# One 128x128 inverse for both heads of a pair: four separate tile chains become one, and the products walk the four 32x32 corners in turn

## Chip, cores and metric

The kernel runs on one core of a Trainium2 chip. The metric is the device time of one execution in microseconds (us); lower is better. TensorE multiplies, VectorE (DVE) and ScalarE (ACT) move and combine tiles, GpSimd (POOL) does small elementwise work, SyncE (SP) issues the DMA transfers. The profile also gives TensorE's granted clock as a share of its upper level: 1.0 is 2.4 GHz and 0.5 is 1.2 GHz.

## The reference, cut to what matters

Two decoder layers on 256 tokens of width 1024. The first one has a Gated DeltaNet mixer with 8 heads, cut into chunks of C tokens (64 in the reference; the kernel takes 128, so a head has two chunks). In every chunk of every head a unit lower triangular matrix is inverted:

```
L = jnp.where(strict, jnp.einsum('bhnid,bhnjd->bhnij', kb, k) * decay, 0.0)
eye = jnp.eye(C, dtype=f32)
T = lax.linalg.triangular_solve(eye + L, jnp.broadcast_to(eye, L.shape),
                                left_side=True, lower=True, unit_diagonal=True)
u = jnp.einsum('bhnij,bhnjd->bhnid', T, v * beta[..., None])
w = jnp.einsum('bhnij,bhnjd->bhnid', T, kb * jnp.exp(gc)[..., None])
```

The rest (causal convolutions, the state that runs from chunk to chunk, memory attention, the ConvGLU, the sparse attention of the second layer) is not touched. All of it is in float32; the large products split each operand into a rounded high part and a low part.

## The kernel before

**How the program comes to its order.** The Python code only records operations; every recorded call has line 389, so the profile is read by tile names and not by lines. The class `Sched` then sets the order on each engine: a list scheduler with a cost for each operation (`_cost`), a priority by place in the code, and a limited number of buffers of each kind. A `with PE.group():` block is one operation to it and stays together. Each engine runs its own list strictly in order; when the count or cost of an operation changes, the lists of all engines may change far around it.

**The work around the inverse.** `gdn_pair(p)` handles two heads (`e` is 0 or 1) with two chunks each (`t` is 0 or 1), for four pairs. Each pair goes through three stages that the list `"dd0dddddd01021321323"` interleaves with those of other pairs: projections, convolution and the matrix `LL` (128x128 for each chunk); the inverse; and the walk over the chunks. `pj` and `pf` are the accumulators of ordinary projections (128x256 products in high and low parts), which the scheduler sets between the dependent steps of a pair. The weights of `pf` (memory keys and values) arrive as `mr`, ScalarE rounds them to `mh`, VectorE makes the rest `ml`.

**The inverse of a 128x128 chunk.** The 16x16 diagonal blocks are inverted row by row on VectorE and GpSimd (`DD`, `tm`), sent through DRAM and come back as `cd`. From there the inverse is built up in three steps, each of two products with a copy between them:

1. 32x32: `D32` holds the inverses of the four 32x32 diagonal blocks, first without their inner corner; two products and one VectorE operation on the result complete them (first product `mx<-D,LL`, `X` is made on VectorE, second product `mx<-D,X` and `mx<-X,D`, the second of these for the transposed copy).
2. 64x64: six ScalarE copies put `D` into the tile `full`; product `mx<-D,LL` (off-diagonal 32x32 blocks), two copies to `X`, product `mx<-X,D` and `mx<-D,X`, three scaled copies into `full`.
3. 128x128: product `mx<-full,LL` (64x64), a copy to `X`, product `mx<-X,full`, a scaled copy into `full`.

Before the change each head has its own `D32`, `X`, accumulators (`p1`, `p2`, tiles `mx`) and its own `full` tile out of four, so a pair has two such chains side by side, 12 groups of products in all. In step 1 the products of one corner come right after one another: two (first product) or four (second product) before the next corner's. After the inverse `mx<-bv,full` begins the third stage. A float32 product stands in the trace as two matmul records. A 32x32 product reads only 32 partitions and writes only 32, so it occupies one 32x32 corner of TensorE's array.

Of the kernel before, what the change touches and what calls it, by code (L numbers as in the profile page):

```python
# [14 lines left out]
OP = mybir.AluOpType  # L15
# [4 lines left out]
P = 128  # L20
S = 256
D = 1024
KD = D // P
FF = 2816
# [10 lines left out]
IB = 16  # L35
# [11 lines left out]
C_ID, C_TRI, C_EYE = 0, 128, 256  # L47
C_BD = C_EYE + IB * IB
# [481 lines left out]
def body(ctx, tc, xT, memT, vecs, consts, rows, relb, w_few, w_in0, w_out0, w_up0, w_dn0, w_in1, w_out1, w_up1, w_dn1,  # L530
# [29 lines left out]
    def Sm(tag, shape, bufs=2):  # L560
        return sc.tile("s", shape, F32, tag, bufs)
# [15 lines left out]
    def mm(*a, **kw):  # L577
        PE.matmul(*a, **kw)
# [103 lines left out]
    def rstd_fin(*accs, keep="row", kept=None):  # L682
# [63 lines left out]
    def mem_attn(layer, h, qmT, rcs=None):  # L746
# [3 lines left out]
        m = Sm("mm", [P, 2])  # L750
        V.tensor_reduce(m, two(pss), axis=AX.X, op=OP.max)
        nm = Sm("mnm", [P, 2])
# [79 lines left out]
    for ch in "wmmimmwxxxxsb0v":  # L832
# [17 lines left out]
        elif ch == "v":  # L850
            vecb = fixed([P, NV - V_GNORM], "vecb")
            cst = fixed([P, C_HOT - C_TRI], "cst")
# [123 lines left out]
            A.activation(g2[:, t], g2[:, t], AF.Exp, bias=gc[:, t, h:h + 1], scale=-1.0)  # L976
        decays.append((g1, g2))

    full = [fixed([P, 3, P], f"full{i}") for i in range(4)]
    for t in full:  # L980
        PO.memset(t, 0.0)

    def gdn_pair(p):
        hd = (2 * p, 2 * p + 1)
        fast, fastz = p > 1, p < H // 2 - 1
        kT, qT, kd, bv, co, AT, LL, DX, ki, cw = {}, {}, {}, {}, {}, {}, {}, {}, {}, {}
        for e, h in enumerate(hd):
# [11 lines left out]
            ss = Sm("ss", [P, 4])  # L999
            V.tensor_reduce(ss, two(sq, 4), axis=AX.X, op=OP.add)  # L1000
            V.tensor_scalar(ss, ss, EPS if fast else 4 * EPS, None, op0=OP.add)
# [26 lines left out]
            for t in range(2):  # L1028
                for j, s in enumerate((kT[e], qT[e])):
                    mm(pgm[:, t * S + j * P:t * S + (j + 1) * P], kT[e][:, t * P:(t + 1) * P], s[:, t * P:(t + 1) * P],  # L1030
                       start=True, stop=True)
# [10 lines left out]
        for e in range(2):  # L1042
            SY.dma_start(sl.raw(lambda r, e=e: bass.AP(tensor=r.tensor, offset=r.offset + 2 * e * US,
                                                      ap=[[P, P], [US, 2], [1, P]]), [P, 2, P]), LL[e])
        Lb = K("Lb", 1, shape=(4 * NB, IB, IB))
        SY.dma_start(Lb, sl.raw(lambda r: bass.AP(tensor=r.tensor, offset=r.offset,
                                                 ap=[[IB * P + IB, 4 * NB], [P, IB], [1, IB]]), [4 * NB, IB, IB]), runs=4 * NB * IB)
# [4 lines left out]
        for k in range(IB - 1):  # L1052
# [3 lines left out]
                             in1=Dm[:, k, :m][:, None, :].to_broadcast([4 * NB, n, m]), op=OP.mult)  # L1056
# [4 lines left out]
                                             ap=[[IB * IB, 4 * NB], [4 * NB * IB * IB, 2], [1, IB * IB]]),  # L1061
                           [4 * NB, 2, IB * IB]), DD.rearrange("p w a b -> p w (a b)"))
        cd = K("cd", 2, shape=(P, 2, 4, IB))
# [1 line left out]
                    sd.raw(lambda r: bass.AP(tensor=r.tensor, offset=r.offset, ap=[[IB, P], [NB * IB * IB, 8], [1, IB]]),  # L1065
                           [P, 8, IB]), runs=8 * P)

        bd = cst[:, C_BD - C_TRI:C_BD + 2 - C_TRI][:, None, :, None].to_broadcast([P, 2, 2, IB])
        quads = [slice(u, u + 32) for u in range(0, P, 32)]
        for e in range(2):  # L1070
            D = DX[e] = K("D32", 4, shape=(P, 2, 2, 32))
            for w in range(2):
                V.tensor_tensor(out=D[:, w].rearrange("p t (c i) -> p t c i", c=2),
                                in0=cd[:, w, 2 * e:2 * e + 2][:, :, None, :].to_broadcast([P, 2, 2, IB]), in1=bd, op=OP.mult)
            p1 = mx()
            with PE.group():
                for u in quads:
                    for t in range(2):
                        mm(p1[u, t * 32:(t + 1) * 32], LL[e][u, t, u], D[u, 1, t], start=True, stop=True)
            X = K("X", 3, shape=(P, 2, 32))  # L1080
            V.tensor_tensor(out=X, in0=two(p1[:, :64]), in1=D[:, 1], op=OP.add)
            p2 = mx()
            with PE.group():
                for u in quads:
                    for t in range(2):
                        mm(p2[u, t * 32:(t + 1) * 32], X[u, t], D[u, 0, t], start=True, stop=True)
                        mm(p2[u, 64 + t * 32:96 + t * 32], D[u, 0, t], X[u, t], start=True, stop=True)
            V.scalar_tensor_tensor(D.rearrange("p w t i -> p (w t i)"), D.rearrange("p w t i -> p (w t i)"), 2.0, p2[:, :P],
                                   op0=OP.mult, op1=OP.subtract)

        for e in range(2):
            D, F = DX[e], full[hd[e] % 4]
            for u in quads:
                A.copy(F[u, :2, u], D[u, 1])
            for u in quads[:2]:
                A.copy(F[u, 2].rearrange("p (t k) -> p t k", t=2)[:, :, u], D[u, 0])
            p1 = mx()
            with PE.group():
                for E, O in (quads[:2], quads[2:]):
                    for t in range(2):  # L1100
                        mm(p1[E, t * 32:(t + 1) * 32], LL[e][O, t, E], D[O, 1, t], start=True, stop=True)
            X = K("X", 3, shape=(P, 2, 32))
            with A.group():
                for E in quads[::2]:
                    A.copy(X[E], two(p1[E, :64]))
            p2 = mx()
            with PE.group():
                for E, O in (quads[:2], quads[2:]):
                    for t in range(2):
                        mm(p2[E, t * 32:(t + 1) * 32], D[E, 0, t], X[E, t], start=True, stop=True)  # L1110
                for t in range(2):
                    E, O = quads[:2]
                    mm(p2[O, t * 32:(t + 1) * 32], X[E, t], D[E, 0, t], start=True, stop=True)
            with A.group():
                for E, O in (quads[:2], quads[2:]):
                    A.mul(F[E, :2, O], two(p2[E, :64]), -1.0)
                E, O = quads[:2]
                A.mul(F[O, 2].rearrange("p (t k) -> p t k", t=2)[:, :, E], two(p2[O, :64]), -1.0)
        for e in range(2):
            F = DX[e] = full[hd[e] % 4]  # L1120
            E, O = slice(0, 64), slice(64, P)
            p1 = mx()
            with PE.group():
                for t in range(2):
                    mm(p1[E, t * 64:(t + 1) * 64], LL[e][O, t, E], F[O, t, O], start=True, stop=True)
            X = K("X", 3, shape=(64, 2, 64))
            A.copy(X, two(p1[E, :P]))
            p2 = mx()
            with PE.group():
                for t in range(2):  # L1130
                    mm(p2[E, t * 64:(t + 1) * 64], F[E, 2, t * 64:(t + 1) * 64], X[:, t], start=True, stop=True)
            A.mul(F[E, :2, O], two(p2[E, :P]), -1.0)

        yield

# [51 lines left out]
    for h in range(1, MH):  # L1187
        mem_k(0, h, wm0, *ms0[:2])
    prs = [gdn_pair(p) for p in range(H // 2)]
    dh = 0  # L1190
    for ch in "dd0dddddd01021321323":
# [49 lines left out]
    for h in range(H):  # L1241
        bt = K("bias", H, shape=(P, 2, P))
        SY.dma_start(bt, sk.raw(lambda r, h=h: bass.AP(tensor=r.tensor, offset=r.offset + h * HOTN + P - 1,
                                                      ap=[[H * HOTN - 1, P], [P, 2], [1, P]]), [P, 2, P]))
# [14 lines left out]
    for j in range(2):  # L1259
        for g in range(G):  # L1260
            ps = proj(w1, (j * 2 + g) * KD, hs)
            t = K("cmpT")
# [6 lines left out]
            c = (j * 2 + g) * NCMP  # L1269
            for i in range(8):  # L1270
# [3 lines left out]
                                op=OP.subtract)  # L1274
# [276 lines left out]
```

## Time and profile before

| | |
|---|---|
| time, median of 3 runs | 806.21 us (806.08, 806.21, 809.37) |
| profiled execution, its own time | 809.9 us |
| its span, first to last instruction | 808.1 us |
| TensorE busy in the span | 787.2 us, 97% |
| VectorE, ScalarE, GpSimd busy | 640.6, 518.7, 142.0 us |
| mean granted clock | 0.989 |

The span leaves out 1.8 us at the ends of the execution. The durations of matmul records overlap (each has a fill and a drain), so the pace of products is read from starts, not from lengths. In a merged row of the timeline the count stands behind x, and the length runs from the first start to the last end.

### The profile page before, as it was taken

What the parts mean: (1) busy time and instruction counts of PE and PEld (TensorE: products, weight loads), DVE (VectorE), ACT (ScalarE), POOL (GpSimd) and SP (SyncE); (2) the same over time, 40 slices, a digit from 0 to 9 for tenths busy, and PEclk for the clock granted to TensorE, in tenths of its full rate; (3) what the DMA queues carried; (4) which work ended last, traced back from release to release, by engine and by line L of the source; (5) the groups of instructions that cost most, each with busy time, mean ns of one, the idle gap of its engine ahead of it and who ended that gap; (6) DMA issues with size and microseconds to landing.
All of it is one profiled execution on the core that took longest, in us unless ns stands there. A gap on an engine that the chain in (4) does not pass through costs nothing.

```text
span 808.1 us, 15329 instructions
## 1 busy us (share of the span) xinstructions
PE 787.2 (97%) x5633; PEld 714.6 (88%) x5633; DVE 640.6 (79%) x1360; ACT 518.7 (64%) x1154; POOL 142.0 (18%) x223
## 2 busy tenths in 40 slices
PE   5999999999999999999999999999999999999995
PEld 5999989999898888888888899999888888888884
DVE  6988958677659898989866687887698989897662
ACT  7579656868764666666543476799646767675340
POOL 1053603352011021221100130000011121212000
PEclk9999979999999999999999999999999999999998
DMA  8575623543415666666656698421365656566641
GB/s 307 216 239 172 180 73 119 170 119 117 130 37 179 207 179 197 184 181 191 192 180 193 191 293 280 151 80 54 108 198 167 200 170 204 177 197 182 196 131 52
DMA packets 52918, 137.22 MB, mean 170 GB/s; under 512 B 11571, under 2 KB 17900, under 8 KB 52716
## 3 DMA queue, kind: packets, MB, share of 16 engines
q1 hardware_dynamic: 52844, 136.26, 55.1%
q8 instruction: 44, 0.72, 0.4%
q14 instruction: 30, 0.25, 0.1%
HBM read 133.86 MB, written 3.95 MB: 171 GB/s over the span
## 4 chain that ended last, share of the span: by engine, by line
PE 90%; DMA 3%; ACT 3%; DVE 2%; issue 1%; SPq 0%; POOL 0%; POOLq 0%; ACTq 0%; DVEq 0%
PE mx L389 66%; PE pj L389 19%; PE pf L389 5%; DMA wr<-in_w_in 1%; ACT full L389 1%; DMA wr<-in_cw 1%; DVE wl L389 1%; ACT wh L389 1%; DMA mt<-in_memT 1%; SPq L389 0%; ACT X L389 0%; POOL rs L389 0%; DVE ln L389 0%; DVE cy L389 0%; POOLq L1546 0%
## 5 line engine op out<-in xcount | busy, mean ns | idle before, releaser
L389 DVE TENSOR_TENSOR wl<-wr,wh 128x1024 fp32r<-128x1024 f32 x224 | 278.4, 1248 | 42.5 <-ACT wh L389 41.6
L389 ACT CAST wh<-wr 128x1024 fp32r<-128x1024 f32 x224 | 232.9, 1046 | 25.7 <-PE mx L389 13.7
L389 PE MATMUL mx<-x,wh 128*128 128x512 f32 x704 | 249.3, 400 | 0.0
L389 PE MATMUL mx<-x,wl 128*128 128x256 f32 x704 | 197.9, 281 | 0.0
L389 PE MATMUL pj<-x,wh 128*128 128x256 f32 x896 | 172.6, 291 | 0.0
L389 PEld LDWEIGHTS mx<-x,wh 128*128 128x128 f32 x704 | 132.4, 188 | 32.7
L389 PEld LDWEIGHTS pj<-x,wh 128*128 128x128 f32 x896 | 139.4, 191 | 2.0 <-issue 0.6
L389 PEld LDWEIGHTS mx<-x,wl 128*128 128x128 f32 x704 | 133.2, 189 | 0.0
L389 PE MATMUL pj<-x,wl 128*128 128x256 f32 x448 | 126.7, 283 | 0.0
L389 PE MATMUL mx<-g,wh 128*128 128x512 f32 x352 | 124.5, 399 | 0.0
L389 PE MATMUL mx<-g,wl 128*128 128x256 f32 x352 | 98.9, 281 | 0.0
L389 PEld LDWEIGHTS pj<-x,wl 128*128 128x128 f32 x448 | 85.5, 191 | 0.0
L389 POOL TENSOR_TENSOR fs<-fs,rs 128x256 f32<-128x256 f32 x44 | 49.7, 1130 | 197.4 <-ACT fs L389 191.6
L389 PEld LDWEIGHTS mx<-g,wh 128*128 128x128 f32 x352 | 66.2, 188 | 16.4
L389 PE MATMUL mx<-mix,wh 128*128 128x512 f32 x192 | 68.3, 401 | 0.0
L389 PEld LDWEIGHTS mx<-g,wl 128*128 128x128 f32 x352 | 66.6, 189 | 0.0
L389 PE MATMUL mx<-mix,wl 128*128 128x256 f32 x192 | 53.6, 279 | 0.0
L389 DVE TENSOR_TENSOR xall<-xall,mx 128x256 f32<-128x256 f32 x64 | 26.8, 419 | 31.8 <-PE mx L389 30.7
L389 ACT COPY half<-mx 128x256 f32<-128x256 f32 x88 | 32.4, 368 | 28.2 <-PE mx L389 26.9
L389 DVE SCALAR_TENSOR_TENSOR fy<-fgr,vecb,fy 128x255 f32<-128x255 f32 x88 | 42.0, 478 | 6.8 <-ACT fy L389 6.8
L389 ACT ACTIVATE x<-xall,vec 128x256 fp32r<-128x256 f32 x24 | 12.2, 510 | 54.7 <-DVE xall L389 54.7
L389 POOL TENSOR_TENSOR sq<-xall 128x256 f32<-128x256 f32 x7 | 9.7, 1386 | 197.5 <-DVE xall L389 197.5
(306 smaller groups left out, 1343.8 us busy)
## 6 DMA issues: line engine op xcount, KB each, us to landing
wr<-in_w_up SPq DMA_DIRECT2D x88, 512.0 KB, 4.4
wr<-in_w_in SPq DMA_DIRECT2D x60, 512.0 KB, 4.4
wr<-in_w_dn SPq DMA_DIRECT2D x44, 512.0 KB, 4.2
wr<-in_w_out SPq DMA_DIRECT2D x24, 512.0 KB, 3.6
mr<-in_w_mem SPq DMA_DIRECT2D x32, 256.0 KB, 4.6
wr<-in_cw SPq DMA_DIRECT2D x8, 512.0 KB, 4.9
mt<-in_memT SPq DMA_DIRECT2D x8, 256.0 KB, 5.0
sk<-skr SPq DMA_DIRECT2D x1, 1536.0 KB, 7.8
```

Source lines behind the costliest of these rows:

```text
L389: i = getattr(getattr(nc, self.eng), m)(*[fix(x) for x in a], **{k: fix(v) for k, v in kw.items()})
```

## The change

The two heads of a pair share one tile at each place: `D32` is 128 x 2 x 4 x 32 (the 4 is head and chunk), `X` and the accumulators hold both heads, and `full` is two tiles of [128, 2 heads, 3, 128] in place of four of [128, 3, 128], taken in turn by the pairs. Each VectorE and ScalarE operation of the three steps is issued once for the pair with twice the elements (one VectorE operation makes all of `D32` where there were four). The products are the same in number and size, 76 for a pair, in 6 groups in place of 12; within a group the loop over head and chunk (`et`) is now the outer one and the loop over corners (`quads`) the inner one. VectorE operations go from 8 to 3 for a pair, ScalarE's from 26 to 13. The diff cut to its core:

```
-    full = [fixed([P, 3, P], f"full{i}") for i in range(4)]
+    full = [fixed([P, 2, 3, P], f"full{i}") for i in range(2)]
...
-        for e in range(2):
-            D = DX[e] = K("D32", 4, shape=(P, 2, 2, 32))
-            for w in range(2):
-                V.tensor_tensor(out=D[:, w].rearrange("p t (c i) -> p t c i", c=2),
-                                in0=cd[:, w, 2 * e:2 * e + 2][:, :, None, :].to_broadcast([P, 2, 2, IB]), in1=bd, op=OP.mult)
-            p1 = mx()
-            with PE.group():
-                for u in quads:
-                    for t in range(2):
-                        mm(p1[u, t * 32:(t + 1) * 32], LL[e][u, t, u], D[u, 1, t], start=True, stop=True)
...
-            p2 = mx()
-            with PE.group():
-                for u in quads:
-                    for t in range(2):
-                        mm(p2[u, t * 32:(t + 1) * 32], X[u, t], D[u, 0, t], start=True, stop=True)
-                        mm(p2[u, 64 + t * 32:96 + t * 32], D[u, 0, t], X[u, t], start=True, stop=True)
...
+        et = [(e, t, slice((2 * e + t) * 32, (2 * e + t + 1) * 32)) for e in range(2) for t in range(2)]
+        D = K("D32", 2, shape=(P, 2, 4, 32))
...
+        p1 = mx()
+        with PE.group():
+            for e, t, c in et:
+                for u in quads:
+                    mm(p1[u, c], LL[e][u, t, u], D[u, 1, 2 * e + t], start=True, stop=True)
+        X = K("X", 3, shape=(P, 4, 32))
+        V.tensor_tensor(out=X, in0=four(p1[:, :P]), in1=D[:, 1], op=OP.add)
+        p2 = mx()
+        with PE.group():
+            for e, t, c in et:
+                for u in quads:
+                    mm(p2[u, c], X[u, 2 * e + t], D[u, 0, 2 * e + t], start=True, stop=True)
+                for u in quads:
+                    mm(p2[u, P + c.start:P + c.stop], D[u, 0, 2 * e + t], X[u, 2 * e + t], start=True, stop=True)
...
+        for u in quads:
+            A.copy(up(u, u), D[u, 1].rearrange("p (e t) k -> p e t k", e=2))
+        for u in quads[:2]:
+            A.copy(low(u, u), D[u, 0].rearrange("p (e t) k -> p e t k", e=2))
...
+        X = K("X", 3, shape=(64, 4, 64))
+        A.copy(X, four(p1[E, :S]))
+        p2 = mx()
+        with PE.group():
+            for e, t, c in et:
+                mm(p2[E, 2 * c.start:2 * c.stop], F[E, e, 2, t * 64:(t + 1) * 64], X[:, 2 * e + t], start=True, stop=True)
+        A.mul(up(E, O), heads(p2[E, :S]), -1.0)
```

The order that the scheduler makes of it differs in many places. First, TensorE in the first pair, second product of step 1 (32x32, accumulator `mx`, operands `D` and `X`). Before, where head 0's last products meet head 1's first (each row one product):

```order
L389 MATMUL mx_1731<-D_244_1679,X_1699 32x32
L389 MATMUL mx_1731<-X_1699,D_244_1679 32x32
L389 MATMUL mx_1750<-D_248_1687,X_1710 32x32
L389 MATMUL mx_1750<-X_1710,D_248_1687 32x32
L389 MATMUL mx_1750<-D_248_1687,X_1710 32x32
```

and now, with the projection in front of it:

```order
L389 MATMUL pf_1620<-mh_1074,mem_131 128x256
L389 MATMUL mx_1675<-D_242_1615,X_1628 32x32 x4
L389 MATMUL mx_1675<-X_1628,D_242_1615 32x32 x4
L389 MATMUL mx_1675<-D_242_1615,X_1628 32x32 x4
L389 MATMUL mx_1675<-X_1628,D_242_1615 32x32 x4
```

The two kinds alternated product by product within one corner; now each kind goes through four corners before the other kind does. Second, TensorE at the end of the first pair's inverse (`pf` is a projection for the second layer's memory keys). Before:

```order
L389 MATMUL mx_1864<-X_1838,full_116_80 64x64 x2
L389 MATMUL mx_1868<-full_117_96,LL_984 64x64 x2
L389 MATMUL pf_1822<-mem_1674,mh_1773 128x256 x2
L389 MATMUL pf_1822<-mem_1674,ml_1814 128x256
L389 MATMUL pf_1822<-mem_1685,mh_1773 128x256 x2
L389 MATMUL pf_1822<-mem_1685,ml_1814 128x256
L389 MATMUL mx_1885<-X_1869,full_117_96 64x64 x2
L389 MATMUL mx_1889<-bv_753,full_116_80 128x128
```

and now:

```order
L389 MATMUL pf_1620<-mh_1657,mem_180 128x256
L389 MATMUL mx_1799<-full_116_80,LL_701 64x64 x2
L389 MATMUL mx_1799<-full_116_80,LL_962 64x64 x2
L389 MATMUL mx_1816<-X_1800,full_116_80 64x64 x4
L389 MATMUL pf_1833<-mem_1649,mh_1814 128x256 x2
L389 MATMUL pf_1833<-mem_1649,ml_1824 128x256
L389 MATMUL mx_1839<-bv_751,full_116_80 128x128
```

The second product of step 3 (`mx<-X,full`) stood with projections of the other head around it and now follows its first product (`mx<-full,LL`) directly, with one block of a projection behind it. Third, ScalarE at the same place. Before, from the first `full` copies on:

```order
L389 COPY full_116_80<-D_244_1679 32x2x32 x6
L389 COPY X_1778<-mx_1777 32x64 x2
L389 COPY full_117_96<-D_248_1687 32x2x32 x5
L389 ACTIVATE full_116_80<-mx_1806 32x2x32 x3
L389 COPY full_117_96<-D_248_1687 32x2x32
L389 COPY X_1784<-mx_1783 32x64 x2
L389 ACTIVATE vm_1338<-pf_1337,rmem_40_288 128x256
L389 COPY X_1838<-mx_1837 64x128
```

and now:

```order
L389 COPY full_116_80<-D_242_1615 32x2x2x32 x6
L389 COPY X_1731<-mx_1730 32x128 x2
L389 ACTIVATE mem_1759<-mt_686,vec_82 128x256
L389 ACTIVATE mem_1765<-mt_686,vec_82 128x256
L389 ACTIVATE mem_1784<-mt_688,vec_82 128x256
L389 ACTIVATE full_116_80<-mx_1767 32x2x2x32 x3
L389 ACTIVATE vm_1611<-pf_1610,rmem_40_284 128x256
L389 ACTIVATE vm_1621<-pf_1620,rmem_40_284 128x256
L389 ACTIVATE mem_1808<-mt_688,vec_82 128x256
L389 COPY X_1800<-mx_1799 64x256
L389 CAST mh_1814<-mr_1673 128x512
```

One set of six copies, two `X` copies and three scaled copies stands where two sets were woven into each other; the last `X` copy now has other work (`vm`, `mem`) in front and the rounding of the next projection's weights (`mh`) behind it.

## Rows read from the trace of the kernel before

**Rows 1.** The page: span, engines (busy, share, instructions), the chain that ended last.
```profile
span 808.1 us, 15329 instructions
PE 787.2 (97%) x5633; PEld 714.6 (88%) x5633; DVE 640.6 (79%) x1360; ACT 518.7 (64%) x1154; POOL 142.0 (18%) x223
...
PE 90%; DMA 3%; ACT 3%; DVE 2%; issue 1%; SPq 0%; POOL 0%; POOLq 0%; ACTq 0%; DVEq 0%
```

**Rows 2.** Busy time by stretch: length, engines (instructions), granted clock, DMA share, GB/s.
```profile
100.00:122.00 22.00, 20.73 (x247) 18.93 (x247) 12.96 (x46) 13.80 (x48) 1.34 (x5) 0.77 0.26 76
178.00:190.00 12.00, 12.00 (x206) 10.25 (x205) 5.52 (x16) 8.92 (x32) 1.92 (x6) 1.00 0.30 73
240.00:780.00 540.00, 539.04 (x3324) 480.34 (x3324) 448.08 (x861) 341.63 (x688) 71.28 (x59) 1.00 0.60 181
```

**Rows 3.** TensorE timeline, third pair: start, length of the merged row, what, count.
```profile
...
177.98 0.40 PE L389 MATMUL pj<-x,wh 128*128 128x256 f32 x2
178.22 0.28 PE L389 MATMUL pj<-x,wl 128*128 128x256 f32 x1
178.43 0.49 PE L389 MATMUL mx<-D,LL 32*32 32x32 f32 x32
178.85 0.50 PE L389 MATMUL pj<-x,wh 128*128 128x256 f32 x2
...
179.40 0.24 PE L389 MATMUL mx<-D,X 32*32 32x32 f32 x2
...
180.68 0.22 PE L389 MATMUL mx<-X,D 32*32 32x32 f32 x2
180.83 0.50 PE L389 MATMUL pj<-x,wh 128*128 128x256 f32 x2
...
181.38 0.32 PE L389 MATMUL mx<-D,LL 32*32 32x32 f32 x8
...
183.51 0.23 PE L389 MATMUL mx<-X,D 32*32 32x32 f32 x2
...
188.12 0.68 PE L389 MATMUL mx<-X,full 64*64 64x64 f32 x8
...
```

**Rows 4.** TensorE timeline, first pair: the two longest waits, in brackets with their releaser.
```profile
...
106.44 0.44 PE L389 MATMUL mx<-X,D 32*32 32x32 f32 x5 [0.72 <-ACT X L389]
...
108.40 0.69 PE L389 MATMUL mx<-full,LL 64*64 64x64 f32 x4 [0.51 <-ACT full L389]
...
```

**Rows 5.** Busy time by stretch around the first pair, columns as in rows 2.
```profile
106.00:108.00 2.00, 1.45 (x18) 1.18 (x18) 1.93 (x6) 1.87 (x9) 0.00 (x0) 1.00 0.12 38
108.00:110.00 2.00, 1.57 (x17) 1.32 (x18) 0.77 (x4) 1.88 (x9) 0.28 (x1) 0.54 0.06 12
110.00:118.00 8.00, 8.00 (x42) 7.32 (x42) 2.58 (x8) 3.79 (x13) 0.59 (x2) 0.50 0.00 0
```

**Rows 6.** ScalarE timeline, first pair, copies in front of the X copies.
```profile
...
104.65 1.51 ACT L389 COPY full<-D 32x64 f32<-32x64 f32 x6
106.18 0.43 ACT L389 COPY X<-mx 32x64 f32<-32x64 f32 x2
...
```

**Rows 7.** ScalarE groups by form, 95 to 225 us: count, busy us, mean ns, idle before.
```profile
L389 ACT COPY full<-D 32x64 f32<-32x64 f32 x48 | 11.6, 242 | 7.3 <-DVE D L389 6.8
...
L389 ACT CAST mh<-mr 128x512 fp32r<-128x512 f32 x14 | 8.7, 621 | 0.0
...
L389 ACT COPY o<-mx 128x128 f32<-128x128 f32 x7 | 1.9, 265 | 2.3 <-PE mx L389 2.2
...
L389 ACT COPY qm<-pj 128x256 f32<-128x256 f32 x4 | 1.5, 377 | 0.0
```

**Rows 8.** VectorE groups by form, 95 to 225 us, columns as in rows 7.
```profile
L389 DVE TENSOR_TENSOR ml<-mr,mh 128x512 fp32r<-128x512 f32 x13 | 8.8, 684 | 8.5 <-ACT mh L389 8.5
...
L389 DVE SCALAR_TENSOR_TENSOR D<-D,mx 128x128 f32<-128x128 f32 x8 | 2.3, 288 | 3.5 <-PE mx L389 3.3
```

**Rows 9.** TensorE, one group by form over the span, columns as in rows 7.
```profile
...
L389 PE MATMUL mx<-X,D 32*32 32x32 f32 x192 | 9.3, 195 | 0.9 <-ACT X L389 0.9
...
```

More of the change, by code (lines that the diff above doesn't have):

```diff
@@ L1066, in gdn_pair @@
                            [P, 8, IB]), runs=8 * P)
-        bd = cst[:, C_BD - C_TRI:C_BD + 2 - C_TRI][:, None, :, None].to_broadcast([P, 2, 2, IB])
+        bd = cst[:, C_BD - C_TRI:C_BD + 2 - C_TRI][:, None, :, None].to_broadcast([P, 8, 2, IB])
         quads = [slice(u, u + 32) for u in range(0, P, 32)]
-        for e in range(2):
-            D = DX[e] = K("D32", 4, shape=(P, 2, 2, 32))
-            for w in range(2):
-                V.tensor_tensor(out=D[:, w].rearrange("p t (c i) -> p t c i", c=2),
-                                in0=cd[:, w, 2 * e:2 * e + 2][:, :, None, :].to_broadcast([P, 2, 2, IB]), in1=bd, op=OP.mult)
-            p1 = mx()
-            with PE.group():
-                for u in quads:
-                    for t in range(2):
-                        mm(p1[u, t * 32:(t + 1) * 32], LL[e][u, t, u], D[u, 1, t], start=True, stop=True)
-            X = K("X", 3, shape=(P, 2, 32))
-            V.tensor_tensor(out=X, in0=two(p1[:, :64]), in1=D[:, 1], op=OP.add)
-            p2 = mx()
-            with PE.group():
-                for u in quads:
-                    for t in range(2):
-                        mm(p2[u, t * 32:(t + 1) * 32], X[u, t], D[u, 0, t], start=True, stop=True)
-                        mm(p2[u, 64 + t * 32:96 + t * 32], D[u, 0, t], X[u, t], start=True, stop=True)
-            V.scalar_tensor_tensor(D.rearrange("p w t i -> p (w t i)"), D.rearrange("p w t i -> p (w t i)"), 2.0, p2[:, :P],
-                                   op0=OP.mult, op1=OP.subtract)
@@ L1091, in gdn_pair @@
-        for e in range(2):
[L1092 to L1132, printed above, removed]
+        et = [(e, t, slice((2 * e + t) * 32, (2 * e + t + 1) * 32)) for e in range(2) for t in range(2)]
@@ new lines, in gdn_pair @@
+        four = lambda ap: two(ap, 4)
+        D = K("D32", 2, shape=(P, 2, 4, 32))
+        V.tensor_tensor(out=D.rearrange("p w u (c i) -> p (w u) c i", c=2),
+                        in0=cd.rearrange("p w u i -> p (w u) i")[:, :, None, :].to_broadcast([P, 8, 2, IB]), in1=bd, op=OP.mult)
+        p1 = mx()
[4 more added lines that the diff above has]
+        X = K("X", 3, shape=(P, 4, 32))
@@ new lines, in gdn_pair @@
+        V.tensor_tensor(out=X, in0=four(p1[:, :P]), in1=D[:, 1], op=OP.add)
[6 more added lines that the diff above has]
+                    mm(p2[u, P + c.start:P + c.stop], D[u, 0, 2 * e + t], X[u, 2 * e + t], start=True, stop=True)
+        V.scalar_tensor_tensor(D.rearrange("p w u i -> p (w u i)"), D.rearrange("p w u i -> p (w u i)"), 2.0, p2[:, :S],
+                               op0=OP.mult, op1=OP.subtract)
@@ new lines, in gdn_pair @@
+        F = full[p % 2]
+        up = lambda r, c: F[r, :, :2, c]
+        low = lambda r, c: F[r, :, 2].rearrange("p e (t k) -> p e t k", t=2)[:, :, :, c]
+        heads = lambda ap: ap.rearrange("p (e t k) -> p e t k", e=2, t=2)
+        for u in quads:
+            A.copy(up(u, u), D[u, 1].rearrange("p (e t) k -> p e t k", e=2))
+        for u in quads[:2]:
+            A.copy(low(u, u), D[u, 0].rearrange("p (e t) k -> p e t k", e=2))
+        p1 = mx()
+        with PE.group():
+            for e, t, c in et:
+                for E, O in (quads[:2], quads[2:]):
+                    mm(p1[E, c], LL[e][O, t, E], D[O, 1, 2 * e + t], start=True, stop=True)
@@ new lines, in gdn_pair @@
+        X = K("X", 3, shape=(P, 4, 32))
+        with A.group():
+            for E in quads[::2]:
+                A.copy(X[E], four(p1[E, :P]))
+        p2 = mx()
+        with PE.group():
+            for e, t, c in et:
+                for E in quads[::2]:
+                    mm(p2[E, c], D[E, 0, 2 * e + t], X[E, 2 * e + t], start=True, stop=True)
+                E, O = quads[:2]
+                mm(p2[O, c], X[E, 2 * e + t], D[E, 0, 2 * e + t], start=True, stop=True)
+        with A.group():
+            for E, O in (quads[:2], quads[2:]):
+                A.mul(up(E, O), heads(p2[E, :P]), -1.0)
+            E, O = quads[:2]
+            A.mul(low(O, E), heads(p2[O, :P]), -1.0)
@@ new lines, in gdn_pair @@
+        E, O = slice(0, 64), slice(64, P)
+        p1 = mx()
+        with PE.group():
+            for e, t, c in et:
+                mm(p1[E, 2 * c.start:2 * c.stop], LL[e][O, t, E], F[O, e, t, O], start=True, stop=True)
+        X = K("X", 3, shape=(64, 4, 64))
+        A.copy(X, four(p1[E, :S]))
+        p2 = mx()
+        with PE.group():
+            for e, t, c in et:
+                mm(p2[E, 2 * c.start:2 * c.stop], F[E, e, 2, t * 64:(t + 1) * 64], X[:, 2 * e + t], start=True, stop=True)
@@ L1134, in gdn_pair @@
+        A.mul(up(E, O), heads(p2[E, :S]), -1.0)
+        for e in range(2):
+            DX[e] = F[:, e]
         yield
```

## The prediction

> **What bounds the kernel now.** I read the page first: TensorE is busy for 787.2 of 808.1 us, and 90% of the chain that ended last lies on it [rows 1]. Then the windows: from 240 us to 780 us TensorE is busy for 539.04 of 540 us at full clock, while VectorE has 92 us and ScalarE 198 us to spare [rows 2]. So a microsecond that TensorE saves while the inverses run (about 100 to 220 us) is not lost behind them: what follows starts earlier and nothing else sets the end. Work taken from VectorE and ScalarE, which the change does too, is worth only what TensorE waits for it.
>
> Third, what the inverse costs TensorE. In the stretch of the third pair TensorE is never idle (12.00 of 12 us), in that of the first it is (20.73 of 22) [rows 2]. So in later pairs the price of the inverse is its own pace and the switching around it, and in the first pair also waits: 0.72 us for `X` and 0.51 us for `full` [rows 4]. And from 108 to 118 us the granted clock is at or near 0.5, the lower level [rows 5]. Before it fell, TensorE was busy for 1.45 of 2 us, with 18 short products [rows 5]. At 0.5 a product takes twice as long, so the lost time is 2 x 0.46 + 8 x 0.50 = 4.9 us.
>
> **Part by part.** *Second product of step 1, corners in turn.* It has 32 products for a pair, 64 records. One record by itself is 0.19 us long, mostly fill and drain [rows 9], so a merged row less 0.19 is the time from its first to its last start. Before, the 64 records run from 179.40 to 180.68 + 0.22 - 0.19 = 180.71: 1.31 us, 20 ns a record [rows 3]. There eight records of one corner stand behind one another. In the first product, where only four do before the corner changes, 32 records need 0.49 - 0.19 = 0.30 us, 9.5 ns each [rows 3]. So corners overlap in time where the order lets them. In turn, with never more than two records of a corner in a row, I take the 9.5 ns: 64 x 9.5 = 0.60 us, 0.71 us less for a pair, 2.8 us for four. Bounds: the eight records over two corners need 0.32 - 0.19 = 0.13 us [rows 3]. That is 16 ns a record (64 x 16 ns = 1.04, saving 0.27 a pair), or, if the two corners ran fully side by side, 32 ns for each record of one corner; with 16 records a corner that is 0.51 us, saving 0.80. So 1.1 to 3.2 us for four pairs. The first product already changes corner after four records, and I give it nothing.
>
> The Trainium skill has a rule that speaks against this term: "TensorE: Matmul & The Clock Gate", section "Wait — 56ns, not 53.3ns?", says that matmuls never start less than about 25 ns apart, however small they are. By that rule, as an estimate, 64 records need 1.6 us in any order and the term is nothing. The 9.5 ns of the first product is below that floor, so this trace disagrees where the corners differ.
>
> *Fewer switches between shapes.* A run of small products costs beside its own pace. The run at 178.43 starts 0.21 us after the projection record before it (178.22), where two projection records are 0.40 - 0.28 = 0.12 us apart; that is 0.09 [rows 3]. At its end the last start is 178.43 + 0.30 = 178.73, and the projection starts at 178.85, 0.12 later [rows 3]. Together 0.21 us. In the third pair there are nine such runs, the first at 178.43 and the last at 188.12 [rows 3]; in the whole order of before there are 33, in that of the change 23 (24 groups, of which two of the first pair adjoin). Ten fewer save 10 x 0.21 = 2.1 us; with only the gap of 0.09 counted, 0.9.
>
> *Copies and combinations.* ScalarE's 26 operations of a pair become 13, VectorE's 8 become 3, each with twice the elements. A six-copy set of 32x64 pieces at 242 ns becomes one of 32x128. The slope from 128x128 (265 ns) to 128x256 (377) is 112 ns for 128 elements, so 64 more cost 56: about 298 ns [rows 7]. Six take 1.79 us; two `X` copies at 0.43 / 2 + 0.056 = 0.27 us take 0.54 [rows 6]. Per pair ScalarE has less to do, but one chain lasts 2.33 us where the first head's lasted 1.51 + 0.43 = 1.94 [rows 6]. The second product of step 2 waits for it. In the third pair it came 2.13 us behind the first one (181.38 to 183.51) with no wait [rows 2, 3]. Now 12, 9, 12 and 12 projection records stand between the two in the four pairs, 1.1 to 1.4 us, with 0.6 us for the first product and its switch: up to 2.0 us. So 0.3 us may be bare in three pairs, and with nine records 0.7 in the second: 1.6 us. VectorE's `D` of 288 ns becomes one operation of at most 2 x 288 [rows 8]; the projections between the groups of step 1 (3 to 14 records, from 0.36 us) cover most of that, as they cover the two of before.
>
> *The end of the first pair's inverse.* The second product of step 3 now stands right behind the first, with ScalarE's `X` copy of 64x256 between them: about 0.38 us [rows 7], all bare. The next projection needs a new `mh` (0.62 us, behind that copy on ScalarE) and its `ml` (0.68 us on VectorE) [rows 7, 8]. The product beside `mh` lasts 0.68 - 0.19 = 0.5 us (the row at 188.12 [rows 3]) and leaves 0.1 bare; two records of 0.12 stand ahead of the one that needs `ml` and leave 0.4. Against these 0.9 us the 1.23 us of before go. Net of all waits: 1.6 + 0.9 - 1.2 = 1.3 us more by the bare sums. Since the copies start when `D` is done, before TensorE comes to the first product, I take half of it, 0.6 us. Bounds: a gain of 1.2, all of them covered, and a loss of 1.3 and rival two's 2.8.
>
> Nothing is moved that has a transfer of the inverse behind it; DMA is at 0.26 to 0.30 of its time here [rows 2].
>
> Sum: 2.8 + 2.1 - 0.6 = 4.3 us less. The profiled execution took 809.9 us, its span and 1.8 us at the ends, so it becomes 805.6. It is 3.7 us above the median of the runs shown, 806.21 us; the terms don't depend on that, so I expect a median of 801.9 us.
>
> **Rivals.** *One: turning through the corners gives nothing*, because the pace is set by something other than the corner (two operands taken in turn as weights). For it: the second product is the only one with two kinds of product, and the only slow one. Against: the kinds of products have the same size. Then 801.9 + 2.8 = 804.7 us.
>
> *Two: the single chain waits.* With two heads woven into each other one's copies lay beneath the other's products; now nothing of the pair is left to fill in. If each copy costs the whole 0.377 us of the large row, six and two of them take 6 x 0.08 + 2 x 0.11 = 0.7 us more a pair, all bare, 2.8 us for four: 804.7 us. For it: both long waits of before have ScalarE as releaser [rows 4]. Against: no such wait in the third pair [rows 2].
>
> *Three: the stretch of low clock falls away.* It began behind waits and short products [rows 5]. If the denser runs of the first pair keep the upper level, 4.9 us come on top, but the runs of 806 us may hold a shorter stretch than the profiled one; 3.7 us separate them, so I count 3.2: 798.7 us.
>
> *Four, slower: more stretches of low clock.* If bare waits in the second to fourth pair let the clock fall as in the first, each costs 4.9 us. One gives 801.9 + 4.9 = 806.8, two give 811.7. It decides from the second one on. For it: the new waits of up to 0.7 us a pair are of the length of those of rows 4. Against: the third pair keeps 1.00 with nine runs of short products [rows 2].
>
> **How the numbers follow.** Less than 0.5% (4 us) a measurement of this kernel can hardly tell from no change; the bounds are 802.2 and 810.2 us. Forecast 0.50 (800 to 803.8; 0.3 of it below 802.2), rival one 0.10, two 0.20, three 0.15, four 0.05 (half of it slower). Faster: 0.30 + 0.15 + 0.05 from the near ends of rivals one and two, 0.50; slower 0.03; same 0.47. The range of 798.0 to 806.0 takes in rival three's time and both ends of the terms, and leaves out rival four, the far end of three and that of rival two's waits.
>
> **What would show it.** In the profile after: 23 runs of small products; the second product of step 1 as one stretch of 64 records with some 0.6 us from first to last start (1.3 would be rival one); TensorE's waits for `X` of at most some 0.3 us a pair (0.7 and more: rival two); the granted clock from 100 to 122 us at 0.77 again (1.00: rival three) and at 1.00 in the later pairs (less: rival four). Wrong it would be most easily by the clock, which I can't derive from the order.

## The result, and the profile after

The changed kernel takes 799.71 us (median of 4 runs, 798.09 to 800.19) beside 807.51 us before (median of 4): a ratio of 0.9899, with an interval of 0.9869 to 0.9928. That is 7.8 us less, where the forecast had 4.3. The profiled execution took 800.06 us, 9.8 less than that of before. The page of the changed kernel, its span, its engines and the chain that ended last:

```profile
span 798.2 us, 15212 instructions
...
PE 776.3 (97%) x5633; PEld 705.2 (88%) x5633; DVE 639.4 (80%) x1344; ACT 511.9 (64%) x1102; POOL 142.6 (18%) x217
...
PE 87%; DMA 4%; DVE 3%; ACT 3%; issue 1%; POOL 1%; SPq 0%; POOLq 0%; DVEq 0%; ACTq 0%
```

TensorE still bounds the kernel; it is busy for 10.9 us less than in [rows 1], with as many products. Where they went, the windows show (columns as in rows 2). First two stretches of the kernel before, then the same two and those around the first pair in the changed one:

```profile
60.00:95.00 35.00, 35.00 (x297) 35.00 (x296) 30.82 (x70) 27.50 (x63) 17.59 (x39) 1.00 0.53 170
100.00:222.00 122.00, 120.23 (x1381) 112.51 (x1380) 87.03 (x255) 88.39 (x269) 32.05 (x77) 0.96 0.41 122
```

```profile
60.00:95.00 35.00, 34.26 (x289) 34.05 (x288) 29.92 (x69) 27.26 (x63) 20.74 (x48) 1.00 0.54 163
100.00:222.00 122.00, 120.23 (x1446) 114.76 (x1446) 93.35 (x256) 88.80 (x243) 35.05 (x81) 1.00 0.43 126
100.00:122.00 22.00, 20.75 (x267) 19.59 (x267) 17.27 (x56) 17.06 (x51) 5.17 (x11) 1.00 0.37 113
106.00:108.00 2.00, 0.90 (x11) 0.59 (x9) 1.07 (x6) 1.96 (x7) 0.57 (x2) 1.00 0.14 48
108.00:110.00 2.00, 1.85 (x16) 1.58 (x17) 1.68 (x5) 1.38 (x4) 0.00 (x0) 1.00 0.00 0
110.00:118.00 8.00, 8.00 (x71) 7.94 (x70) 6.01 (x26) 5.42 (x19) 1.20 (x3) 1.00 0.03 8
```

Three things stand there. (The granted clock of before is still 0.90 from 118 to 120 us, which [rows 5] leave out.) In the stretch of the inverses (100 to 222 us) TensorE's idle time is 1.77 us before and after: the waits balance to nothing. In the stretch ahead of them (60 to 95 us) 0.74 us of idle time is new. And from 100 to 122 us the granted clock is 1.00 where it was 0.77 [rows 2]: the low clock that the forecast counted at 4.9 us [rows 5] is gone, although TensorE is busy for only 0.90 us of the two from 106 to 108.

The timeline of TensorE in the third pair (columns as in rows 3) shows the second product of step 1:

```profile
...
168.34 0.28 PE L389 MATMUL pj<-x,wl 128*128 128x256 f32 x1
168.54 0.45 PE L389 MATMUL mx<-D,LL 32*32 32x32 f32 x32
168.93 0.50 PE L389 MATMUL pj<-x,wh 128*128 128x256 f32 x2
...
169.62 0.28 PE L389 MATMUL pj<-x,wl 128*128 128x256 f32 x1
169.83 0.26 PE L389 MATMUL mx<-D,X 32*32 32x32 f32 x8
...
170.34 0.24 PE L389 MATMUL mx<-X,D 32*32 32x32 f32 x6
170.51 0.44 PE L389 MATMUL mx<-ident,o 128*128 128x128 f32 x2
...
```

The 64 records go from 169.83 to 170.51, where the next product starts: 0.68 us. Before, from 179.40 to 180.83, it was 1.43 [rows 3]. From first to last start they take 170.34 + 0.24 - 0.19 - 169.83 = 0.56 us, 8.8 ns a record. All four pairs show 0.56, so this is 4 x 0.75 = 3.0 us less. The first product, too, is a little faster: 0.45 where 0.49 stood. Each run of small products still starts 0.20 us behind the record before it (168.34 to 168.54), where two projection records are 0.12 us apart. There are 23 runs where there were 33.

ScalarE's and VectorE's operations of doubled width, by form (columns as in rows 7):

```profile
L389 ACT COPY full<-D 32x128 f32<-32x128 f32 x24 | 7.1, 297 | 4.3 <-DVE D L389 4.1
...
L389 ACT COPY X<-mx 32x128 f32<-32x128 f32 x8 | 2.0, 255 | 0.2
...
L389 ACT COPY X<-mx 64x256 f32<-64x256 f32 x4 | 1.5, 364 | 0.1
```

```profile
...
L389 DVE SCALAR_TENSOR_TENSOR D<-D,mx 128x256 f32<-128x256 f32 x4 | 1.7, 416 | 0.9 <-PE mx L389 0.9
...
```

The six copies cost 297 ns each (298 was estimated), the `X` copies 255 (270 estimated); `D` takes 416 and not twice 288.

### The profile page after: what moved, and what is told of

It reads as the page before. It is cut to its first block, busy times and chain, and to the rows that moved or that the text cites. A ratio compares the mean times of both kernels' runs of the same rounds, so it can differ in the third digit from the quotient of the medians.

```text
span 798.2 us, 15212 instructions
## 1 busy us (share of the span) xinstructions
PE 776.3 (97%) x5633; PEld 705.2 (88%) x5633; DVE 639.4 (80%) x1344; ACT 511.9 (64%) x1102; POOL 142.6 (18%) x217
## 4 chain that ended last, share of the span: by engine, by line
PE 87%; DMA 4%; DVE 3%; ACT 3%; issue 1%; POOL 1%; SPq 0%; POOLq 0%; DVEq 0%; ACTq 0%
PE mx L389 67%; PE pj L389 17%; PE pf L389 4%; DMA wr<-in_w_in 2%; DVE wl L389 1%; DMA sk<-skr 1%; ACT g L389 1%; DMA mt<-in_memT 1%; ACT wh L389 1%; DMA bias<-sk 1%; DVE cy L389 0%; ACT full L389 0%; DVE ml L389 0%; ACT mh L389 0%; SPq L389 0%
```

## Experiments

The time varies from execution to execution by up to 6.5 us for one kernel, so each mechanism is read from rows, and the times beside them. The mean granted clock of each execution is known; a table of it closes this section. It is a rough measure: each profiled execution also ends with 5 to 8 us at the lower level, when TensorE has hardly any work left, and that alone moves the mean by up to 0.002.

**One half of the change alone.** First the order of the corners in the kernel before, each head by itself:

```
-                for u in quads:
-                    for t in range(2):
-                        mm(p2[u, t * 32:(t + 1) * 32], X[u, t], D[u, 0, t], start=True, stop=True)
-                        mm(p2[u, 64 + t * 32:96 + t * 32], D[u, 0, t], X[u, t], start=True, stop=True)
+                for t in range(2):
+                    for u in quads:
+                        mm(p2[u, t * 32:(t + 1) * 32], X[u, t], D[u, 0, t], start=True, stop=True)
+                    for u in quads:
+                        mm(p2[u, 64 + t * 32:96 + t * 32], D[u, 0, t], X[u, t], start=True, stop=True)
```

> The kernel before with one edit: in the second product of step 1 each head's products walk the four corners in turn, the tiles of the two heads stay apart. The order on every engine is otherwise that of before. Theory: 64 records take 0.56 us where they took 1.32, so four pairs save 3.0 us, and no switch is saved: about 804.5 us beside a before of 807.5. The low clock of the first pair comes from the waits of steps 2 and 3, which are still there, so it falls to 0.5 again near 107 us. Rival one (corner order gives nothing; the gain is that of merging): no change, 807.5 us. Rival two (the slow second product itself brings the low clock): 3.0 us for the pace and up to 4.9 us for the clock, about 800 us, with the granted clock at 1.00 from 100 to 122 us.

Measured: 809.86 us beside 809.08, ratio 1.0006 (0.9993 to 1.0019). No gain, though the pace is there. The third pair's second product in its timeline, two rows:

```profile
...
178.03 0.26 PE L389 MATMUL mx<-D,X 32*32 32x32 f32 x8
...
178.71 0.39 PE L389 MATMUL pj<-x,wh 128*128 128x256 f32 x1
...
```

From 178.03 to the projection at 178.71 it takes 0.68 us, as in the change. So rival one falls by its mechanism (the corners do give 0.75 us a pair) and is right by its time. Rival two falls too: with the fast product the clock from 100 to 122 us is still at 0.84. Where the 3.0 us went, the waits of TensorE from 100 to 220 us show (total, times, longest), of this kernel and of before, and the longest one in the timeline:

```profile
PE mx L389 <- ACT X L389: 2.3, 3, 1.5
```

```profile
PE mx L389 <- ACT X L389: 1.1, 3, 0.7
PE mx L389 <- ACT full L389: 0.5, 1, 0.5
```

```profile
...
107.73 0.25 PE L389 MATMUL mx<-X,D 32*32 32x32 f32 x1 [1.48 <-ACT X L389]
...
```

TensorE comes earlier to the second product of step 2, and ScalarE, with its 26 operations a pair in the same order as before, doesn't. The wait of 0.72 us in the first pair [rows 4] is 1.48 us. The waits grew by 0.7 us (2.3 against 1.1 + 0.5). And the median of the mean granted clock is 0.987 where before has 0.989, which would be up to 0.002 x 806 = 1.6 us more lost to low clock. Together that is at most 2.3 of the 3.0 us; the rest I could not place. The two parts come from different executions: the profiled one, at 0.992, has less low clock than before's (0.84 from 100 to 122 us against 0.77). So the growth of the waits is shown, and the part of the clock is only argued.

Second, the merging alone: the changed kernel with its second product of step 1 corner after corner.

```
-            for e, t, c in et:
-                for u in quads:
-                    mm(p2[u, c], X[u, 2 * e + t], D[u, 0, 2 * e + t], start=True, stop=True)
-                for u in quads:
-                    mm(p2[u, P + c.start:P + c.stop], D[u, 0, 2 * e + t], X[u, 2 * e + t], start=True, stop=True)
+            for u in quads:
+                for e, t, c in et:
+                    mm(p2[u, c], X[u, 2 * e + t], D[u, 0, 2 * e + t], start=True, stop=True)
+                    mm(p2[u, P + c.start:P + c.stop], D[u, 0, 2 * e + t], X[u, 2 * e + t], start=True, stop=True)
```

> The changed kernel with one edit: the second product of step 1 has its products corner after corner again, 16 records of a corner in a row. The order on every engine is otherwise that of the change. Theory: it loses the 0.75 us a pair of the corners (or a little more, since 16 records of a corner now stand in a row where 8 did), 3.0 us: about 802.7 us, and keeps the 10 fewer switches and the clock at 1.00 in the first pair. Rival one (corner order gives nothing): 799.7 us. Rival two (the slow second product brings the low clock): 3.0 + 4.9 us, about 807 us, with the granted clock at 0.5 for some 10 us behind the first pair's second product.

Measured: 805.05 us, ratio 0.9949 (0.9936 to 0.9962), 4.0 us less than before and 2.9 more than the changed kernel on the same chip. Its window of the first pair:

```profile
100.00:122.00 22.00, 20.89 (x248) 19.95 (x247) 15.08 (x53) 14.98 (x44) 3.63 (x9) 0.92 0.29 86
```

The clock is at 0.92 there, between 0.77 and 1.00. So merging brings most of the clock's gain. Whether the slow second product brings a piece of low clock back is not shown: this execution has the lowest mean clock of the six (0.993; the others 0.994 to 0.996), and over all six the clock is no lower than the changed kernel's (table below). But the kernel with four orders (next part), whose second product in the first pair is slow too, shows the same:

```profile
100.00:122.00 22.00, 20.75 (x275) 19.57 (x267) 15.29 (x50) 15.56 (x46) 3.10 (x8) 0.92 0.29 92
```

By rows the 16 records of a corner in a row cost more than the 3.0 us expected: 1.84 us (from 100.07 to 101.91 in the first pair) where the change takes 0.68, so 4.6 us for four pairs. The times show 2.9; some executions of the changed kernel lost time elsewhere, as the next run shows. Third, the changed kernel again beside these two:

> The changed kernel itself, beside the two kernels that hold one half of the change each. All theories: about 8 us less than before (799.7 beside 807.5). What is open is whether the granted clock of the first pair stays at 1.00 in each execution, or is an accident of some of them.

Measured: 802.12 us beside 809.08, ratio 0.9906 (0.9887 to 0.9925). The clock was 0.991 to 0.995 in its executions; none is as low as the median of before, 0.989. The profiled one (0.992) had no low clock from 100 to 122 us; its loss lies far ahead of the change, from 20 to 40 us, where the clock is 0.86 and before's is 1.00. That the first pair keeps 1.00 in the executions without a profile is likely by their means, and not shown.

**What sets the pace of small products.** The changed kernel, with the second product of step 1 written in a different order in each pair:

```
+            if p == 0:
+                for u in quads:
+                    for i in et:
+                        first(u, *i)
+                for u in quads:
+                    for i in et:
+                        second(u, *i)
+            elif p == 1:
+                for i in et:
+                    for u in quads:
+                        first(u, *i)
+                        second(u, *i)
...
```

> The changed kernel, with the second product of step 1 written in another order in each pair. Pair 1: one kind of product alone, 8 records of a corner in a row, then the other kind. Pair 2: both kinds alternate, but the corner changes after 4 records. Pair 3: kinds alternate, 8 records of a corner in a row (as before the change). Pair 4: kinds alternate, 16 records of a corner in a row. Theory (the corner sets the pace): from first to last start of the 64 records, pair 1 and pair 3 take 1.3 us alike, pair 2 0.6 to 0.65 (as the first product with its 4 in a row), pair 4 1.3 or more. Rival (the two kinds that alternate as weights set it): pair 1 takes 0.6, pairs 2 to 4 1.3 us.

Its timeline, for each pair the first row of the 64 records and the first product behind them:

```profile
...
101.85 0.24 PE L389 MATMUL mx<-D,X 32*32 32x32 f32 x2
...
103.28 0.38 PE L389 MATMUL pf<-mh,mem 128*128 128x256 f32 x1
...
135.27 0.24 PE L389 MATMUL mx<-D,X 32*32 32x32 f32 x3
...
136.05 0.39 PE L389 MATMUL pj<-x,wh 128*128 128x256 f32 x1
...
173.45 0.21 PE L389 MATMUL mx<-D,X 32*32 32x32 f32 x1
...
174.89 0.33 PE L389 MATMUL mx<-ident,o 128*128 128x128 f32 x1
...
201.84 0.24 PE L389 MATMUL mx<-D,X 32*32 32x32 f32 x2
...
203.68 0.39 PE L389 MATMUL pf<-mem,mh 128*128 128x256 f32 x1
...
```

One kind alone, 8 records of a corner in a row: 101.85 to 103.28, 1.43 us. Both kinds, the corner changing after 4 records: 135.27 to 136.05, 0.78 us. Both kinds, 8 in a row: 1.44. Both kinds, 16 in a row: 1.84. The theory holds: the number of records of one corner in a row sets the pace, the kinds that alternate don't. Less the 0.12 us to the next product, that is 10 ns a record with 4 in a row, 20 with 8 and 27 with 16. (804.64 us, one execution.)

**Why the clock stayed up.** First the kernel before, with fillers in the first pair and nothing else changed:

```
             with PE.group():
+                if p == 0:
+                    for _ in range(2):
+                        PE._g.calls.append(("matmul", (p2[:, S:S + P], ident, ones), dict(start=True, stop=True)))
                 for E, O in (quads[:2], quads[2:]):
...
             with PE.group():
+                if p == 0:
+                    for _ in range(2):
+                        PE._g.calls.append(("matmul", (p1[:, S:S + P], ident, ones), dict(start=True, stop=True)))
                 for t in range(2):
```

> The kernel before with fillers in the first pair only: in front of the second product of step 2 and of the first product of step 3 TensorE makes two 128x128 float32 products of constants each into unused columns, which wait for nothing. Eight products of some 0.25 us, 2.0 us in all, of which the waits of 0.72 and 0.51 us hide 1.2. The order on every engine is otherwise that of before. Theory: the granted clock falls in the first pair because TensorE stands there or does short products. With the fillers it stays at 1.00 from 100 to 122 us, 4.9 us less for the clock and 0.8 more for bare fillers: about 804.5 us beside a before of 808.5. Rival (the stretch of low clock has another cause): the clock falls to 0.5 near 108 us again, and the time is 0.8 us above before.

Measured: 806.48 us beside 808.88, ratio 0.9972 (0.9957 to 0.9988). Its windows:

```profile
106.00:108.00 2.00, 1.94 (x25) 1.67 (x24) 1.83 (x8) 1.88 (x9) 0.00 (x0) 1.00 0.02 5
108.00:110.00 2.00, 2.00 (x27) 1.64 (x26) 0.28 (x2) 1.85 (x9) 0.28 (x1) 1.00 0.03 8
112.00:118.00 6.00, 6.00 (x53) 5.80 (x53) 3.19 (x13) 3.45 (x11) 0.80 (x3) 1.00 0.00 0
100.00:122.00 22.00, 21.85 (x288) 20.05 (x288) 14.77 (x53) 16.42 (x56) 2.47 (x8) 1.00 0.25 74
```

The clock is 1.00 throughout, and over 12 executions 0.994 to 0.997, where 18 of before lie between 0.986 and 0.991. So what TensorE does there, its waits and short products, brings the low clock of the first pair, not another cause. The time fell by 2.4 us and not by 4. Two things explain it. The low clock costs less than was reckoned. The same 30 records, from a projection (`pf<-mem,mh`) to `mx<-Sx,kT`, without a wait, in before and in this kernel (columns as in rows 2):

```profile
111.92:118.11 6.19, 6.19 (x30) 5.85 (x29) 1.85 (x7) 2.81 (x9) 0.59 (x2) 0.50 0.00 0
```

```profile
111.37:114.86 3.49, 3.49 (x30) 3.29 (x29) 1.63 (x7) 2.12 (x7) 0.59 (x2) 1.00 0.00 0
```

At the lower level they take 1.77 times as long, not twice, so the whole stretch (2 x 0.46 + 8 x 0.50 + 2 x 0.10 = 5.1 us by halves) costs by that ratio 5.1 x 2.70 / 3.10 = 4.5 us. And the fillers cost more than the 0.8 us that I gave them: the first two groups of four records lie in the two waits, but the last two stand where before doesn't wait. From `mx<-full,LL` to `mx<-Sx,kT` before takes 118.11 - 108.40 = 9.71 us and this kernel 114.86 - 107.81 = 7.05, so 2.66 us are left of some 4.3 that the clock gives back there by the same ratio, and some 1.7 went to fillers (an estimate).

Second and third, the change for the first pair alone and for the other three alone, by one condition around the old and the new text (with two of the small buffers fewer, for room):

```
+        if p == 0:
...
+        else:
...
```

> The change for the first pair alone; the other three pairs have the code of before (two of the small buffers fewer, to make room). Theory (the clock's part of the gain is the first pair's): 0.75 us for the corners, 0.2 for one switch, and some 4.4 us for the clock: about 803 us beside 808.5. Rival (the low clock does not depend on how the first pair is written): 1 us less, about 807.5 us, with some 10 us of 0.5 near 108 us as before.

Measured: 811.04 us, ratio 1.003 (1.0015 to 1.0045): slower than before. The theory as I wrote it falls. Two rows of its timeline in the first pair, and its windows behind them:

```profile
...
105.71 0.44 PE L389 MATMUL mx<-D32m,LL 32*32 32x32 f32 x16 [0.29 <-ACT mh L389]
...
108.03 0.24 PE L389 MATMUL mx<-X,D32m 32*32 32x32 f32 x2 [0.68 <-ACT X L389]
...
```

```profile
108.00:110.00 2.00, 1.94 (x31) 1.79 (x32) 0.50 (x3) 1.40 (x5) 0.29 (x1) 0.76 0.11 35
110.00:112.00 2.00, 2.00 (x13) 1.66 (x12) 1.01 (x3) 0.50 (x2) 0.40 (x2) 0.50 0.00 0
112.00:118.00 6.00, 6.00 (x31) 5.66 (x31) 2.20 (x8) 1.36 (x4) 0.49 (x2) 0.50 0.00 0
```

With the other pairs' code beside it the scheduler sets the first pair's steps differently. TensorE waits 0.29 us and 0.68 us, and then the clock is at 0.50 again. So the merged form of the first pair alone doesn't keep the clock up. That the order around its steps does is argued from these waits; no run changes that order alone, and the two missing buffers are another difference. Why this kernel is slower than before, a window near the end of the fourth pair shows in part:

```profile
195.00:222.00 27.00, 25.70 (x299) 23.59 (x298) 18.01 (x55) 21.34 (x72) 3.42 (x7) 0.94 0.45 140
```

A second stretch of low clock stands there, 0.94 where before has 1.00, behind a wait of 0.8 us for `full`. That is what rival four of the prediction feared for the change.

> The change for the second to fourth pair; the first has the code of before (two of the small buffers fewer). Theory: three times 0.75 us for the corners and 9 switches of 0.21 us, 4.1 us less, and the stretch of low clock in the first pair stays: about 804.4 us beside 808.5. Rival (the later pairs gain by corners and switches what waits give back, as the run with the corners alone did): no change, 808.5 us.

Measured: 804.52 us, ratio 0.9953 (0.9937 to 0.997): 4.4 us less, where 4.1 was expected. The window of the first pair:

```profile
100.00:122.00 22.00, 20.73 (x248) 19.06 (x242) 11.95 (x45) 13.68 (x48) 2.49 (x8) 0.77 0.16 51
```

The clock is at 0.77 as before the change, although two small buffers are missing here too. So this is the gain without the clock: three pairs' corners and nine switches together (24 runs of small products where there were 33). The interval holds 2.4 to 5.1 us, so neither term is shown by itself.

**The wait that the change made.** The longest wait of the changed kernel on TensorE, and ScalarE's timeline ahead of it:

```profile
...
108.01 0.27 PE L389 MATMUL mx<-X,full 64*64 64x64 f32 x1 [1.11 <-ACT X L389]
...
```

```profile
...
106.48 0.84 ACT L389 ACTIVATE vm<-pf,rmem 128x256 f32<-128x256 f32 x2
107.20 0.51 ACT L389 ACTIVATE mem<-mt,vec 128x256 fp32r<-128x256 f32 x1
107.60 0.35 ACT L389 COPY X<-mx 64x256 f32<-64x256 f32 x1
...
```

The prediction gave the `X` copy of the first pair's step 3 0.38 us, all bare. Two `vm` operations and a `mem` operation stand in front of it on ScalarE, 0.84 and 0.51 us, and the wait is 1.11. The edit, in the changed kernel:

```
-        A.copy(X, four(p1[E, :S]))
+        (V.tensor_copy if p == 0 else A.copy)(X, four(p1[E, :S]))
```

> The changed kernel with one edit: in the first pair VectorE and not ScalarE copies X for the second product of step 3. In the change that copy stood behind two vm operations and one mem operation of ScalarE, and TensorE waited 1.11 us for it. VectorE is free there. Theory: the wait falls to about the copy and its way, 0.5 us, so 0.6 us less than the change; by time that is too small to tell, the trace shows it. Rival (something else holds the product): the wait stays at 1.1 us.

Measured: 803.29 us, ratio to before 0.993 (0.9906 to 0.9955): no better than the changed kernel. Its timeline:

```profile
...
109.45 0.65 PE L389 MATMUL mx<-X,full 64*64 64x64 f32 x8 [0.60 <-DVE tm L389]
111.03 0.71 PE L389 MATMUL mx<-bv,full 128*128 128x128 f32 x4 [0.93 <-ACT full L389]
111.50 0.36 PE L389 MATMUL pf<-mem,mh 128*128 128x256 f32 x1
...
```

The wait for `X` fell from 1.11 to 0.60 us, as expected (the row names `tm`, the operation of VectorE behind the copy; the copy itself takes 0.42 us). But with the other cost the order changed too: the projection block that stood behind the product now stands behind the next one, and `mx<-bv,full` waits 0.93 us for `full` (ScalarE rounds two `mh` ahead of it). The wait was moved, not removed: from 100 to 222 us TensorE is idle for 3.19 us, against 1.77 in the changed kernel.

Mean granted clock of the timed executions, lowest, median and highest:

| kernel | executions | clock | median us |
|---|---|---|---|
| before, beside the first three | 17 | 0.988, 0.989, 0.991 | 809.08 |
| corners alone | 12 | 0.986, 0.987, 0.992 | 809.86 |
| merged, old corner order | 6 | 0.993, 0.994, 0.996 | 805.05 |
| changed kernel, again | 6 | 0.991, 0.9935, 0.995 | 802.12 |
| before, beside the last four | 18 | 0.986, 0.989, 0.991 | 808.88 |
| before with fillers | 12 | 0.994, 0.995, 0.997 | 806.48 |
| first pair merged | 7 | 0.986, 0.988, 0.988 | 811.04 |
| later pairs merged | 6 | 0.988, 0.989, 0.990 | 804.52 |
| `X` on VectorE, first pair | 6 | 0.992, 0.995, 0.996 | 803.29 |

A mean of 0.995 where 0.989 stood is 0.006 x 806 = 4.8 us less lost to low clock, if a record takes twice as long there; rows 5 give the same for the stretch, and the 30 records above put it at 4.5.

## Why the prediction was right, point by point

The forecast was 801.9 us in a range of 798.0 to 806.0; 799.7 lies in it, below the likeliest case by a term that the forecast had put among its rivals. The range reaches so far down because it takes in rival three's time, 798.7. The forecast's own terms, 4.3 us less, give 803.2 us from the 807.5 measured for before. That the likeliest case is only 2.2 us off is partly luck, since it started from 806.2.

**The bound.** Right: what TensorE saved before 222 us came out at the end; from 240 to 780 us it is idle for 0.96 us before and 1.17 after.

**Corners in turn.** Right, and a little small: 8.8 ns a record where 9.5 was taken, 3.0 us for 2.8. The pace of the first product was the right row to take it from. The rule of 25 ns between starts ("TensorE: Matmul & The Clock Gate" in the Trainium skill, section "Wait — 56ns, not 53.3ns?") doesn't hold for products on different corners: 8.8 ns here. Where 16 records of one corner stand in a row, 1.84 us less the 0.12 at the end is 27 ns a record: there the trace agrees.

**Switches.** The count is right, 23 runs, and so is the reading of one, 0.20 us ahead of a run as before; 2.1 us is worked out from these and was not measured alone. The later pairs alone gave 4.4 us for three pairs' corners and nine switches (2.2 + 1.9).

**Waits.** I took 0.6 us more; the stretch of the inverses shows none. The six copies cost what was estimated, but the waits of 0.3 to 0.7 us in every pair that I reckoned from them did not come: two waits stand there, 1.11 us in the first pair and 0.52 us in the fourth, and of the 0.5 us reckoned for `mh` and `ml` at most 0.15 came (TensorE is busy for 1.85 of the 2 us from 108 to 110). The first was mis-sized, 0.38 for 1.11, by leaving out what stands in front of the copy on ScalarE, although the order showed it. By the prediction's own sign (0.7 us and more for `X`) rival two is there in the first pair and in no other; in the sum it changes nothing, since the two waits of before, 1.23 us, are gone. The prediction had no term ahead of the inverses; there the new order brings 0.74 us (1.35 in the other profile of the changed kernel), the longest row of it:

```profile
...
67.28 0.39 PE L389 MATMUL pj<-x,wh 128*128 128x256 f32 x1 [0.74 <-ACT kd L389]
...
```

**The clock.** This is the step that failed in size. The forecast kept the low clock of the first pair, and rival three, with 0.15, let it fall away. It fell away, in both executions of the changed kernel that were profiled. The size, 4.9 us, was a little high: the prediction took a product at 0.5 to last twice as long, where the 30 records show 1.77 times, and it left out 118 to 120 us; both together make 4.5.

By terms of the profiled pair: 3.0 + 2.1 + 4.5 for corners, switches and clock, less 0.7 for the new wait, is 8.9 of the 9.8 us. The medians differ by less, 7.8 and, with more executions, 7.0 us. The starts of the executions vary by 2 us or so, and one profile of the changed kernel had a stretch of low clock long before the inverses, from 18.7 us on (the 0.86 above), which before's profile lacks; I can't resolve more than that.

What stays open is which feature of the changed order holds the clock up. Idle time alone doesn't decide: the changed kernel stands for 1.1 us in one piece and keeps 1.00, while waits of 0.29 and 0.68 us with short products between them lost it. The slow second product may matter as well: with the same wait of 1.1 us in the first pair, the two kernels that have it show 0.92.

## What to carry to other kernels

Small products on separate corners of the array overlap well only if the corner changes often in the order (8.8 ns a record with 2 in a row, 10 with 4, 20 with 8, 27 with 16); write the loop over corners as the inner one, and check the pace of starts rather than lengths. A faster step helps only when the step behind it is ready: the same reordering was worth 2.9 us in the merged kernel, and nothing in the kernel before, where longer waits for ScalarE took at least 0.7 us of it back. A stretch of low granted clock can be worth as much as the edit itself (4.5 us beside 5.1 here), so look for it first, ask what TensorE did just before it fell, and give its disappearance a real chance when the change touches that place.

## What was unexpected of the hardware

Useless products brought time: 16 records of fillers in the first pair raised the mean granted clock to 0.994 or more in 12 of 12 executions, from 0.989, and made the kernel 2.4 us faster. And the merged form of the first pair kept the clock or lost it with the code of the other pairs (and two small buffers fewer): a median of 0.9935 with all pairs merged, 0.988 with the first alone. At the lower level, half the clock, the same 30 records took 1.77 times as long and not twice.
